# Score products on unpadded queries in four row groups, with the softmax of a half task re-cut, in a two-layer encoder on one Trainium2 core

## The chip, the cores and the metric

The kernel runs on one core of one Trainium2 chip (trn2). The metric is device time in microseconds of one execution. A run of the kernel gives one time; the time before is the median of three runs.

## The reference, cut to what matters

All of it is in float32. The trunk has two layers over 256 tokens (4 rows of 64) with 2048 channels; the change lies in the attention of the first.

```python
def neighbourhood_attention(h, w_qkv, b_qkv, w_o, rpb):
    qkv = (h @ w_qkv + b_qkv).reshape(B, S, 3, N_HEADS, HEAD_DIM)   # 64 heads of 32
    q = qkv[:, :, 0] * (HEAD_DIM ** -0.5)
    ...
    def row_block(r):                                               # 4 rows of 64 queries
        ...
        bias = rpb[:, dr_idx[None, :, None], dc_idx[:, None, :]]
        s = jnp.einsum('bqhd,bkhd->bhqk', qb, kb) + bias[None]
        s = jnp.where(mask[None, None], s, neg)                     # 16 columns around the query
        pr = jax.nn.softmax(s, axis=-1)
        return jnp.einsum('bhqk,bkhd->bqhd', pr, vb)
    ...
    return o @ w_o

def reference(x, p, ...):
    for i in range(DEPTH):                                          # 2
        if i % 2 == 0: x = x + neighbourhood_attention(rms_norm(x, ...), ...)
        else:          x = x + multiscale_pool(rms_norm(x, ...), ...)
        x = x + swiglu(rms_norm(x, ...), ...)                       # D_FF 5632
        gate = sigmoid(rms_norm(x, ...) @ w_ple_gate[i] + b_ple_gate[i])
        x = x + (p[i] @ w_ple_proj[i]) * gate
    return rms_norm(x, final_norm_g)
```

## The kernel before, in words

Activations lie transposed, channels on the 128 partitions and the 256 tokens along the free axis. To keep float32 accuracy on TensorE, each activation and each weight is split into a high and a low part (`at`, `wh`, `wl`), and `product` (from line 326) multiplies high by both parts of the activation (512 columns, L336) and low by the high one (256 columns, L340).

Weights stream from HBM in chunks of 1 MB on SP's queue, into three raw buffers. `Weights.make` (L94, L95) turns a chunk into two halves of `wh` (a cast on ScalarE) and `wl` (a subtraction on VectorE). There are four slots for halves, so two chunks; `get` makes sure that the two chunks after the one in use are made. All large products take their chunks in one fixed order.

The attention goes through four groups g of 16 heads. For each group `qk` computes queries and keys (eight chunks), `v_proj` the values (four chunks), and from g = 1 on `out_proj(g - 1)` adds the group before to x (four chunks); `out_proj(3)` comes last. A group's 16 heads are four tasks f of four heads j. The 256 queries are taken in four blocks b of 64 (4 rows by 16 columns), each against a window of 4 rows by 32 columns of keys, so 128 keys.

The small work of a task hangs between the chunks. `Side` is a queue of functions, each with a count of steps to let pass; `product` makes a step after every accumulator (8 pairs of products), `v_proj` after every 12 products. `queue_scores` puts the four `scores` tasks between the products of `v_proj`; `queue_attend` puts the transposes of the probabilities (`prob_t`) and the products with the values (`attend`) between the products that follow: of `qk(1, 0)` for g = 0, of `out_proj(g - 1)` for the others.

In `scores` a query tile `qz_f` holds for each head j the 128 channels of f with all but head j's 32 rows zero (filled with zeros once, L409; four activations of 32 partitions write the diagonal, L444). For each pair pr of blocks eight products (L496) go to one PSUM bank of the pool `pt` (`tmp_ps`, two buffers, shared with the transposes and the attend outputs): the two blocks in the two halves of the partitions, the four heads side by side. GpSimd adds bias and mask (L490, four additions, two buffers); VectorE adds them to the scores (L501), takes the maximum (L505) and the reciprocal of the sum (L512); ScalarE takes the exponential with the sum beside it (L508); GpSimd scales (L513). Accumulators of the large products (`acc`) are a pool of their own: three buffers of two PSUM banks.

Which instruction stands where on an engine is decided by the Tile framework's scheduler, by priority and dependence; `urgent()` raises the priority of what is issued within it. Each engine then works through its list in order.

Of the kernel before, what the change touches and what calls it, by code (L numbers as in the profile page):

```python
# [8 lines left out]
F32 = mybir.dt.float32  # L9
# [5 lines left out]
P = 128  # L15
# [115 lines left out]
def tile_encoder(  # L131
# [251 lines left out]
    def attention(nxt):  # L383
# [43 lines left out]
        def qk(g, kind):  # L427
# [26 lines left out]
        def v_proj(g):  # L454
# [17 lines left out]
            for t in range(2):  # L472
                nc.vector.scalar_tensor_tensor(v[:, t, :], a[:, t, :], norm.rows[:, t : t + 1], vb, ALU.mult, ALU.add)
# [9 lines left out]
        def scores(g, f, pr):  # L483
            rb = rb_tiles[g]
            bm = ap2.tile([P, 4, 4, 32], F32, tag="bm", name=f"bm_{g}_{f}_{pr}")
            off = 8 if pr == 0 else 0
            base = rb[:, f * 4 : f * 4 + 4, off : off + 1]
            for j in range(4):
                w1 = bass.AP(tensor=base.tensor, offset=base.offset + j * RUN, ap=[list(base.ap[0]), [31, 4], [1, 32]])
                nc.gpsimd.tensor_tensor(bm[:, j], w1, mask[:, pr : pr + 1, :].broadcast_to([P, 4, 32]), ALU.add)  # L490
            sp = tmp_ps(f"s_{g}_{f}_{pr}")
            for j in range(4):
# [433 lines left out]
```

## Time and profile before

| | us |
|---|---|
| three runs | 2183.17, 2184.16, 2184.46 |
| median | 2184.16 |
| profiled execution, its own time | 2185.78 |
| its span, first to last instruction | 2184.0 |

| engine | busy, share of the span |
|---|---|
| TensorE (PE) | 98% |
| weight load into it (PEld) | 86% |
| VectorE (DVE) | 62% |
| ScalarE (ACT) | 50% |
| GpSimd (POOL) | 9% |

The granted TensorE clock is 0.995 of full speed on average. The attention fills the first 440 us or so, a fifth of the span; the rest is the two feed-forward stages, the gated embeddings and the pooling mixer, which the change does not touch. In a profile PE's busy time counts pipelined products that overlap, so within a stage the distance from one start to the next tells more than the length of one instruction. Times below are microseconds from the span's start.

### The profile page before, as it was taken

What the parts mean: (1) busy time and instruction counts of PE and PEld (TensorE: products, weight loads), DVE (VectorE), ACT (ScalarE), POOL (GpSimd) and SP (SyncE); (2) the same over time, 40 slices, a digit from 0 to 9 for tenths busy, and PEclk for the clock granted to TensorE, in tenths of its full rate; (3) what the DMA queues carried; (4) which work ended last, traced back from release to release, by engine and by line L of the source; (5) the groups of instructions that cost most, each with busy time, mean ns of one, the idle gap of its engine ahead of it and who ended that gap; (6) DMA issues with size and microseconds to landing.
All of it is one profiled execution on the core that took longest, in us unless ns stands there. A gap on an engine that the chain in (4) does not pass through costs nothing.

```text
span 2184.0 us, 32133 instructions
## 1 busy us (share of the span) xinstructions
PE 2148.2 (98%) x13092; PEld 1874.3 (86%) x13092; DVE 1355.8 (62%) x1561; ACT 1088.0 (50%) x1554; POOL 185.7 (9%) x274
## 2 busy tenths in 40 slices
PE   7999999999999999999999999999999999999997
PEld 6888888888888888888888888888888888888887
DVE  5756575876555555566566677556555555556676
ACT  6665656654444434444445566444443344444453
POOL 3424132100000000000003100000000000000013
PEclk9999999999999999999999999999999999999999
DMA  8666565465555555555555454555555555555553
GB/s 243 183 190 190 180 180 174 155 205 191 193 184 184 191 192 184 184 192 192 186 184 184 171 193 141 187 185 183 193 193 183 184 192 193 183 185 192 193 174 116
DMA packets 209443, 402.92 MB, mean 184 GB/s; under 512 B 7936, under 2 KB 20352, under 8 KB 209296
## 3 DMA queue, kind: packets, MB, share of 16 engines
q1 hardware_dynamic: 206000, 393.38, 54.5%
q0 software_dynamic: 2192, 6.49, 1.6%
q8 instruction: 102, 1.67, 0.3%
q10 hardware_dynamic: 1104, 1.02, 0.1%
q14 instruction: 45, 0.37, 0.0%
HBM read 394.56 MB, written 2.10 MB: 182 GB/s over the span
## 4 chain that ended last, share of the span: by engine, by line
PE 95%; POOL 1%; DMA 1%; DVE 1%; issue 1%; ACT 1%; SPq 0%; POOLq 0%; DVEq 0%; ACTq 0%
PE ff L336 30%; PE ff L340 15%; PE dn L336 15%; PE dn L340 8%; PE qk L336 5%; PE pl L336 4%; PE qk L340 3%; PE pl L340 2%; PE wo L336 2%; PE v L466 1%; PE s L496 1%; PE v L468 1%; PE v L467 1%; PE wo L340 1%; PE wo L355 1%; PE ptp L522 1%
## 5 line engine op out<-in xcount | busy, mean ns | idle before, releaser
L95 DVE TENSOR_TENSOR wl<-raw,wh 128x1024 fp32r<-128x1024 f32 (+1 forms) x740 | 904.3, 1229 | 638.6 <-ACT wh L94 637.4
L94 ACT CAST wh<-raw 128x1024 fp32r<-128x1024 f32 (+1 forms) x740 | 768.7, 1043 | 806.5 <-PE ff L336 300.5
L336 PE MATMUL ff<-at_f,wh 128*128 128x512 f32 x2816 | 986.2, 394 | 0.0
L340 PE MATMUL ff<-at_f,wl 128*128 128x256 f32 x2816 | 790.4, 281 | 0.0
L336 PEld LDWEIGHTS ff<-at_f,wh 128*128 128x128 f32 x2816 | 529.6, 188 | 121.8
L340 PEld LDWEIGHTS ff<-at_f,wl 128*128 128x128 f32 x2816 | 530.3, 188 | 0.4 <-DVE wl L95 0.2
L336 PE MATMUL dn<-ht,wh 128*128 128x512 f32 x1408 | 493.0, 394 | 0.0
L340 PE MATMUL dn<-ht,wl 128*128 128x256 f32 x1408 | 395.3, 281 | 0.0
L336 PEld LDWEIGHTS dn<-ht,wh 128*128 128x128 f32 x1408 | 264.8, 188 | 61.1
L340 PEld LDWEIGHTS dn<-ht,wl 128*128 128x128 f32 x1408 | 265.1, 188 | 0.0
L336 PE MATMUL qk<-at_attn,wh 128*128 128x512 f32 x512 | 183.9, 402 | 12.1 <-ACT wh L94 6.5
L336 PE MATMUL pl<-at_p,wh 128*128 128x512 f32 x448 | 158.5, 397 | 0.0
L340 PE MATMUL qk<-at_attn,wl 128*128 128x256 f32 x512 | 144.9, 284 | 0.0
L340 PE MATMUL pl<-at_p,wl 128*128 128x256 f32 x448 | 126.3, 282 | 1.7 <-DVE wl L95 1.7
L336 PEld LDWEIGHTS qk<-at_attn,wh 128*128 128x128 f32 x512 | 97.7, 191 | 34.5 <-ACT wh L94 12.4
L336 PEld LDWEIGHTS pl<-at_p,wh 128*128 128x128 f32 x448 | 84.8, 189 | 19.4
L340 PEld LDWEIGHTS qk<-at_attn,wl 128*128 128x128 f32 x512 | 97.9, 191 | 1.7 <-DVE wl L95 1.2
L370 DVE TENSOR_TENSOR join_ff<-ff,lo_ff 128x512 f32<-128x512 f32 x88 | 60.4, 686 | 54.1 <-ACT lo_ff L368 54.1
L368 ACT COPY lo_ff<-ff 128x512 f32<-128x512 f32 x88 | 51.3, 583 | 81.9 <-PE ff L340 81.9
L304 POOL TENSOR_TENSOR tiny<-tiny 128x2 f32<-128x2 f32 x7 | 9.2, 1315 | 923.5 <-DVE tiny L302 923.5
L340 PEld LDWEIGHTS pl<-at_p,wl 128*128 128x128 f32 x448 | 84.9, 190 | 2.1 <-DVE wl L95 2.1
L490 POOL TENSOR_TENSOR bm<-rb,mask 128x128 f32<-128x128 f32 x128 | 67.6, 563 | 207.9 <-DVE p L501 174.7
(170 smaller groups left out, 1727.6 us busy)
## 6 DMA issues: line engine op xcount, KB each, us to landing
raw<-in_w_gate_dram SPq DMA_DIRECT2D x88, 1024.0 KB, 5.0
raw<-in_w_up_dram SPq DMA_DIRECT2D x88, 1024.0 KB, 5.0
raw<-in_w_down_dram SPq DMA_DIRECT2D x88, 1024.0 KB, 4.9
raw<-in_w_qkv_dram SPq DMA_DIRECT2D x46, 1024.0 KB, 5.2
raw<-in_w_ple_gate_dram SPq DMA_DIRECT2D x32, 1024.0 KB, 4.9
raw<-in_w_o_dram SPq DMA_DIRECT2D x16, 1024.0 KB, 4.9
rb<-in_rpb_dram POOLq DMA_DIRECT2D x32, 133.0 KB, 7.0
vw<-v SPq DMA_DIRECT2D x64, 64.0 KB, 2.7
```

Source lines behind the costliest of these rows:

```text
L94: self.nc.scalar.copy(wh[:, z], r)
L95: self.nc.vector.tensor_tensor(wl[:, z], r, wh[:, z].bitcast(F32), ALU.subtract)
L336: nc.tensor.matmul(a[:, f, :], lhsT=wh[:, k % per, c], rhs=v.rearrange("p a s -> p (a s)"), start=(first and k == 0), stop=False,)
L340: nc.tensor.matmul(a[:, f, :S], lhsT=wl[:, k % per, c], rhs=v[:, 0, :], start=False, stop=(last and k == nk - 1),)
L355: nc.tensor.matmul(o, lhsT=w[:, k % per, c], rhs=v[:, h, :], start=(first and k == 0 and n == 0), stop=(last and k == nk - 1 and n == 2),)
L368: nc.scalar.copy(lo, a[:, :, S:])
L370: nc.vector.tensor_tensor(s, a[:, :, :S], lo, ALU.add)
L466: nc.tensor.matmul(a[:, t, :], lhsT=hi, rhs=wh[:, k % 2, :], start=first, stop=False)
L467: nc.tensor.matmul(a[:, t, :], lhsT=hi, rhs=wl[:, k % 2, :], start=False, stop=False)
L468: nc.tensor.matmul(a[:, t, :], lhsT=lo, rhs=wh[:, k % 2, :], start=False, stop=last)
L490: nc.gpsimd.tensor_tensor(bm[:, j], w1, mask[:, pr : pr + 1, :].broadcast_to([P, 4, 32]), ALU.add)
L496: nc.tensor.matmul(sp[blk * 64 : blk * 64 + 64, j * P : (j + 1) * P], lhsT=qz[f][:, j, b * 64 : (b + 1) * 64], rhs=kv, start=True, stop=True,)
```

## The change

Queries are kept without padding: `qT_f` is one tile of 128 channels by 256, written by one activation, and a head's score product reads only its 32 partitions of `qT` and `kT`. `scores` issues all 16 products of a task at once, into two accumulators from `acc` (two heads each, a bank per head, both pairs of blocks side by side in the bank). The softmax runs per half task h (two heads, all four blocks) instead of per pair of blocks. Bias and mask take two additions of 256 elements, one for each pair of blocks, in four buffers. The additions to the scores, and those that make v, are urgent. Of the four score tasks the first waits for no step, where it waited for one; the transposes wait for four steps instead of two.

```diff
-        qz = []
-        for f in range(4):
-            z = ap_.tile([P, 4, S], F32, name=f"qz_{f}")
-            nc.gpsimd.memset(z, 0.0)
-            qz.append(z)
-        kT = [None] * 4
+        qT, kT = [None] * 4, [None] * 4
...
                     if kind == 0:
-                        for j in range(4):
-                            pr = slice(j * HD, (j + 1) * HD)
-                            nc.scalar.activation(
-                                qz[f][pr, j, :].rearrange("p (b r c) -> p r b c", b=4, r=4),
-                                reversed_last(sm[pr, f2, :].rearrange("p (r b c) -> p r b c", r=4, b=4)), AF.Identity,
-                                bias=bq_s[pr, b : b + 1], scale=float(HD) ** -0.5,
-                            )
+                        qt_ = ap_.tile([P, S], F32, tag=f"qT{f}", name=f"qT_{g}_{f}")
+                        nc.scalar.activation(
+                            qt_.rearrange("p (b r c) -> p r b c", b=4, r=4),
+                            reversed_last(sm[:, f2, :].rearrange("p (r b c) -> p r b c", r=4, b=4)), AF.Identity,
+                            bias=bq_s[:, b : b + 1], scale=float(HD) ** -0.5,
+                        )
+                        qT[f] = qt_
...
-            for t in range(2):
+            with urgent():
+              for t in range(2):
                 nc.vector.scalar_tensor_tensor(v[:, t, :], a[:, t, :], norm.rows[:, t : t + 1], vb, ALU.mult, ALU.add)
...
-        def scores(g, f, pr):
+        def scores(g, f):
             rb = rb_tiles[g]
...
-            sp = tmp_ps(f"s_{g}_{f}_{pr}")
-            for j in range(4):
+            sp = [acc(f"s_{g}_{f}_{h}") for h in range(2)]
+            for pr in range(2):
                 for blk in range(2):
                     b = 2 * pr + blk
-                    kv = kT[f].rearrange("p (r c) -> p r c", r=4)[:, :, KEY_LO[b] : KEY_LO[b] + 32]
-                    nc.tensor.matmul(
-                        sp[blk * 64 : blk * 64 + 64, j * P : (j + 1) * P], lhsT=qz[f][:, j, b * 64 : (b + 1) * 64],
-                        rhs=kv, start=True, stop=True,
-                    )
...
+                    for j in range(4):
+                        rows = slice(j * HD, (j + 1) * HD)
+                        kv = kT[f][rows].rearrange("p (r c) -> p r c", r=4)[:, :, KEY_LO[b] : KEY_LO[b] + 32]
+                        nc.tensor.matmul(
+                            sp[j // 2][blk * 64 : blk * 64 + 64, j % 2, pr * P : (pr + 1) * P],
+                            lhsT=qT[f][rows, b * 64 : (b + 1) * 64], rhs=kv, start=True, stop=True,
+                        )
+            for h in range(2):
+                softmax(g, f, h, sp[h], rb)
+
+        def softmax(g, f, h, sp, rb):
+            bm = ap2.tile([P, 2, 2, 4, 32], F32, tag="bm", bufs=4, name=f"bm_{g}_{f}_{h}")
+            n = f * 4 + h * 2
+            for p2 in range(2):
...
+                nc.gpsimd.tensor_tensor(bm[:, :, p2], near, ok, ALU.add)
+            s = ap3.tile([P, 4, P], F32, tag="prob", name=f"p_{g}_{f}_{h}")
+            with urgent():
+                nc.vector.tensor_tensor(
+                    s.rearrange("p (j b) k -> p j (b k)", j=2), sp[:, :, :S],
+                    bm.rearrange("p j b r c -> p j (b r c)"), ALU.add,
+                )
...
         def queue_scores(g):
             for f in range(4):
-                side.add(lambda f=f: (scores(g, f, 0), scores(g, f, 1)), 1)
+                side.add(lambda f=f: scores(g, f), 0 if f == 0 else 1)
...
-                side.add(lambda f=f: task(f), 2 if f == 0 else 0)
+                side.add(lambda f=f: task(f), 4 if f == 0 else 0)
```

`attend` now takes its probabilities from the half task of the head (`pv[j // 2]`) and goes through the blocks in the same order as before.

How instructions move, at three places. Names end with the group, the task and the half; the last number is a buffer's. First TensorE where the first score task of group 0 stands between the products for v. Before:

```order
L466 MATMUL v_0_662<-wh_8_1_564,at_attn_1_179 128x512
L467 MATMUL v_0_662<-wl_8_1_565,at_attn_1_179 128x512
L468 MATMUL v_0_662<-wh_8_1_564,at_attn_1_179 128x512
L496 MATMUL s_0_0_0_702<-kT_0_0_647,qz_0_226 64x128 x8
L496 MATMUL s_0_0_1_728<-kT_0_0_647,qz_0_226 64x128 x8
L466 MATMUL v_0_662<-wh_9_0_602,at_attn_2_184 128x512
L467 MATMUL v_0_662<-wl_9_0_603,at_attn_2_184 128x512
L468 MATMUL v_0_662<-wh_9_0_602,at_attn_2_184 128x512
```

Now:

```order
L461 MATMUL v_0_646<-wh_8_0_544,at_attn_0_162 128x512
L462 MATMUL v_0_646<-wl_8_0_545,at_attn_0_162 128x512
L463 MATMUL v_0_646<-wh_8_0_544,at_attn_0_162 128x512
L490 MATMUL s_0_0_0_669<-kT_0_0_631,qT_0_0_434 64x128 x5
L490 MATMUL s_0_0_1_670<-kT_0_0_631,qT_0_0_434 64x128 x4
L490 MATMUL s_0_0_0_669<-kT_0_0_631,qT_0_0_434 64x128
L490 MATMUL s_0_0_1_670<-kT_0_0_631,qT_0_0_434 64x128 x2
L490 MATMUL s_0_0_0_669<-kT_0_0_631,qT_0_0_434 64x128 x2
L490 MATMUL s_0_0_1_670<-kT_0_0_631,qT_0_0_434 64x128 x2
L461 MATMUL v_0_646<-wh_8_1_548,at_attn_1_179 128x512
L462 MATMUL v_0_646<-wl_8_1_549,at_attn_1_179 128x512
L463 MATMUL v_0_646<-wh_8_1_548,at_attn_1_179 128x512
```

The block stands 12 products of v earlier (before the second half of the chunk instead of after it), and its products change between the two accumulators of the halves; in the first task of a group the first five go to one of them. In the tasks f = 1 to 3 they change after every two, in the order of the loops.

Second VectorE through the second task of group 0, with the weight subtractions (`wl`) between. Before:

```order
L95 TENSOR_TENSOR wl_11_0_752<-raw_11_749,wh_11_0_751 128x1024
L95 TENSOR_TENSOR wl_11_1_756<-raw_11_749,wh_11_1_755 128x1024
L501 TENSOR_TENSOR p_0_1_0_797<-s_0_1_0_788,bm_0_1_0_783 128x512
L501 TENSOR_TENSOR p_0_1_1_823<-s_0_1_1_814,bm_0_1_1_809 128x512
L505 TENSOR_REDUCE mx_0_1_0_799<-p_0_1_0_797 128x4
L505 TENSOR_REDUCE mx_0_1_1_825<-p_0_1_1_823 128x4
L512 RECIPROCAL rc_0_1_0_806<-sm_0_1_0_801 128x4
L512 RECIPROCAL rc_0_1_1_832<-sm_0_1_1_827 128x4
```

Now:

```order
L511 TENSOR_TENSOR p_0_1_0_772<-s_0_1_0_751,bm_0_1_0_769 128x512
L511 TENSOR_TENSOR p_0_1_1_787<-s_0_1_1_752,bm_0_1_1_784 128x512
L95 TENSOR_TENSOR wl_11_0_732<-raw_11_729,wh_11_0_731 128x1024
L516 TENSOR_REDUCE mx_0_1_0_774<-p_0_1_0_772 128x4
L516 TENSOR_REDUCE mx_0_1_1_789<-p_0_1_1_787 128x4
L95 TENSOR_TENSOR wl_11_1_736<-raw_11_729,wh_11_1_735 128x1024
L523 RECIPROCAL rc_0_1_0_781<-sm_0_1_0_776 128x4
L523 RECIPROCAL rc_0_1_1_796<-sm_0_1_1_791 128x4
```

The two additions to the scores come first, and one of the two weight subtractions has moved between the maxima and the reciprocals.

Third TensorE at the end of the attention, around the last attend (`o_3_3`). Before:

```order
L336 MATMUL wo_2_3_0_4352<-oT_2_1_3008,wh_59_1_4151 128x512
L340 MATMUL wo_2_3_0_4352<-oT_2_1_3008,wl_59_1_4152 128x256
L535 MATMUL o_3_3_4380<-pT_3_3_0_4320,vw_3_4076 32x64 x8
L535 MATMUL o_3_3_4380<-pT_3_3_1_4346,vw_3_4076 32x64 x8
L336 MATMUL wo_2_3_1_4353<-oT_2_0_3007,wh_59_0_4147 128x512
L340 MATMUL wo_2_3_1_4353<-oT_2_0_3007,wl_59_0_4148 128x256
L336 MATMUL wo_2_3_1_4353<-oT_2_0_3007,wh_59_0_4147 128x512
```

Now:

```order
L533 MATMUL ptp_3_3_1_4285<-ident_60,p_3_3_1_3945 128x128 x4
L355 MATMUL wo_3_0_0_4315<-oT_3_0_3989,wh_60_0_4091 128x256 x2
L355 MATMUL wo_3_0_0_4315<-oT_3_0_3989,wl_60_0_4092 128x256
L355 MATMUL wo_3_0_0_4315<-oT_3_1_3990,wh_60_1_4095 128x256
L355 MATMUL wo_3_0_1_4316<-oT_3_0_3989,wh_60_0_4091 128x256 x2
L545 MATMUL o_3_3_4296<-pT_3_3_0_4264,vw_3_3972 32x64 x2
...
L545 MATMUL o_3_3_4296<-pT_3_3_1_4290,vw_3_3972 32x64 x2
L355 MATMUL wo_3_0_1_4316<-oT_3_0_3989,wl_60_0_4092 128x256
L355 MATMUL wo_3_0_1_4316<-oT_3_0_3989,wh_60_0_4091 128x256 x2
L355 MATMUL wo_3_0_0_4315<-oT_3_1_3990,wh_60_1_4095 128x256
```

It has moved from among the products of `out_proj(2)` (`wo_2`) to among the first products of `out_proj(3)` (`wo_3`).

## Rows read from the trace of the kernel before

**Rows 1.** The page: span, and busy time of each engine.
```profile
span 2184.0 us, 32133 instructions
...
PE 2148.2 (98%) x13092; PEld 1874.3 (86%) x13092; DVE 1355.8 (62%) x1561; ACT 1088.0 (50%) x1554; POOL 185.7 (9%) x274
```
**Rows 2.** The page: the chain that ended last, its shares by engine.
```profile
PE 95%; POOL 1%; DMA 1%; DVE 1%; issue 1%; ACT 1%; SPq 0%; POOLq 0%; DVEq 0%; ACTq 0%
```
**Rows 3.** Waits of PE, 0 to 560 us: total us, times, longest.
```profile
PE qk L336 <- ACT wh L94: 6.5, 1, 6.5
PE qk L336 <- DVE at_attn L255: 5.6, 1, 5.6
PE wo L340 <- issue: 1.8, 2, 1.2
PE ptp L522 <- ACT pT L524: 1.0, 4, 0.2
```
**Rows 4.** The chain in order of time: start us, us, what.
```profile
68.43 1.90 PE s L496 x32
...
115.45 0.58 PE o L535 x32
...
386.67 1.90 PE s L496 x32
...
458.96 0.45 PE bps_f L311 x4
```
**Rows 5.** Timeline, end of group 0's keys: start us, us, instruction.
```profile
62.61 0.28 PE L340 MATMUL qk<-at_attn,wl 128*128 128x256 f32 x1
...
65.37 0.68 DVE L370 TENSOR_TENSOR join_qk<-qk,lo_qk 128x512 f32<-128x512 f32 x1
```
**Rows 6.** Busy time by stretch: v stages of groups 0 and 3.
```profile
core 0: us, PE busy (x) PEld busy (x) DVE busy (x) ACT busy (x) POOL busy (x), PEclk, DMA share, GB/s
62.70:93.20 30.50, 30.50 (x226) 24.53 (x224) 21.09 (x31) 19.67 (x62) 18.40 (x31) 1.00 0.51 170
...
358.00:388.50 30.50, 30.50 (x227) 24.51 (x225) 21.15 (x31) 19.60 (x62) 18.27 (x30) 1.00 0.45 154
```
**Rows 7.** Groups of instructions, 0 to 560 us: busy us, mean ns, idle before.
```profile
L444 ACT ACTIVATE qz<-join_qk,cols 32x256 f32<-32x256 f32 x64 | 32.4, 506 | 1.6 <-DVE join_qk L437 0.8
L496 PE MATMUL s<-kT,qz 128*64 128x128 f32 x512 | 31.5, 276 | 0.0
L496 PEld LDWEIGHTS s<-kT,qz 128*64 128x64 f32 x512 | 27.6, 137 | 5.8 <-issue 5.8
```
**Rows 8.** Timeline of GpSimd at the start.
```profile
5.25 3.63 POOL L409 MEMSET qz<- 128x1024 f32 x4
```
**Rows 9.** Timeline of VectorE, second task of group 0; in brackets the idle time before.
```profile
76.19 2.58 DVE L95 TENSOR_TENSOR wl<-raw,wh 128x1024 fp32r<-128x1024 f32 x2 [0.76 <-ACT wh L94]
78.69 1.28 DVE L501 TENSOR_TENSOR p<-s,bm 128x512 f32<-128x512 f32 x2
79.89 1.26 DVE L505 TENSOR_REDUCE mx<-p 128x4 f32<-128x512 f32 x2
82.41 0.18 DVE L512 RECIPROCAL rc<-sm 128x4 f32<-128x4 f32 x1 [1.26 <-ACT p L508]
83.95 0.18 DVE L512 RECIPROCAL rc<-sm 128x4 f32<-128x4 f32 x1 [1.36 <-ACT p L508]
```
**Rows 10.** Timeline of ScalarE, second task: first exponential, and the casts after the eighth.
```profile
80.65 0.40 ACT L508 ACTIVATE p<-p,mx 128x128 f32<-128x128 f32 x1 [3.44 <-DVE mx L505]
...
83.75 1.98 ACT L94 CAST wh<-raw 128x1024 fp32r<-128x1024 f32 x2
```
**Rows 11.** Groups of instructions, 0 to 560 us: what follows transposes and attend.
```profile
L524 ACT COPY pT<-ptp 128x512 f32<-128x512 f32 x32 | 18.2, 582 | 15.8 <-PE ptp L522 15.8
...
L545 DVE TENSOR_TENSOR oT<-o,oT 128x256 fp32r<-128x256 f32 x16 | 6.7, 417 | 3.8 <-ACT oT L544 3.6
L544 ACT CAST oT<-o 128x256 fp32r<-128x256 f32 x16 | 6.0, 373 | 9.3 <-PE o L535 9.3
```

More of the change, by code (lines that the diff above doesn't have):

```diff
@@ L481, in attention @@
         probs = {}
-        def scores(g, f, pr):
+        def scores(g, f):
             rb = rb_tiles[g]
-            bm = ap2.tile([P, 4, 4, 32], F32, tag="bm", name=f"bm_{g}_{f}_{pr}")
-            off = 8 if pr == 0 else 0
-            base = rb[:, f * 4 : f * 4 + 4, off : off + 1]
-            for j in range(4):
-                w1 = bass.AP(tensor=base.tensor, offset=base.offset + j * RUN, ap=[list(base.ap[0]), [31, 4], [1, 32]])
-                nc.gpsimd.tensor_tensor(bm[:, j], w1, mask[:, pr : pr + 1, :].broadcast_to([P, 4, 32]), ALU.add)
-            sp = tmp_ps(f"s_{g}_{f}_{pr}")
-            for j in range(4):
+            sp = [acc(f"s_{g}_{f}_{h}") for h in range(2)]
+            for pr in range(2):
@@ L493, in scores @@
                 for blk in range(2):
                     b = 2 * pr + blk
-                    kv = kT[f].rearrange("p (r c) -> p r c", r=4)[:, :, KEY_LO[b] : KEY_LO[b] + 32]
-                    nc.tensor.matmul(
-                        sp[blk * 64 : blk * 64 + 64, j * P : (j + 1) * P], lhsT=qz[f][:, j, b * 64 : (b + 1) * 64],
-                        rhs=kv, start=True, stop=True,
-                    )
-            s = ap3.tile([P, 4, P], F32, tag="prob", name=f"p_{g}_{f}_{pr}")
-            nc.vector.tensor_tensor(
-                s, sp.rearrange("p (j k) -> p j k", j=4), bm.rearrange("p j a b -> p j (a b)"), ALU.add
-            )
@@ L504, in scores @@
-            mx = aps.tile([P, 4], F32, tag="mx", name=f"mx_{g}_{f}_{pr}")
+                    for j in range(4):
[5 more added lines that the diff above has]
+                        )
@@ new lines, in scores @@
+            for h in range(2):
[4 more added lines that the diff above has]
+            for p2 in range(2):
+                off = 8 if p2 == 0 else 0
+                base = rb[:, n : n + 1, off : off + 1]
+                near = bass.AP(
+                    tensor=base.tensor, offset=base.offset, ap=[list(base.ap[0]), [RUN, 2], [31, 4], [1, 32]]
+                )
+                ok = mask[:, p2 : p2 + 1, :].unsqueeze(1).broadcast_to([P, 2, 4, 32])
+                nc.gpsimd.tensor_tensor(bm[:, :, p2], near, ok, ALU.add)
[4 more added lines that the diff above has]
+                    bm.rearrange("p j b r c -> p j (b r c)"), ALU.add,
+                )
+            mx = aps.tile([P, 4], F32, tag="mx", name=f"mx_{g}_{f}_{h}")
@@ L505, in scores @@
             nc.vector.tensor_reduce(mx, s, AX.X, ALU.max, negate=True)
-            sm = aps.tile([P, 4], F32, tag="sm", name=f"sm_{g}_{f}_{pr}")
+            sm = aps.tile([P, 4], F32, tag="sm", name=f"sm_{g}_{f}_{h}")
             for j in range(4):
@@ L510, in scores, with prob_t @@
                 )
-            rc = aps.tile([P, 4], F32, tag="rc", name=f"rc_{g}_{f}_{pr}")
+            rc = aps.tile([P, 4], F32, tag="rc", name=f"rc_{g}_{f}_{h}")
             nc.vector.reciprocal(rc, sm)
             nc.gpsimd.tensor_tensor(s, s, rc.unsqueeze(2).broadcast_to([P, 4, P]), ALU.mult)
-            probs[f, pr] = s
+            probs[f, h] = s
         prob_ts = {}
-        def prob_t(g, f, pr):
-            s = probs.pop((f, pr))
-            tp = tmp_ps(f"ptp_{g}_{f}_{pr}")
+        def prob_t(g, f, h):
+            s = probs.pop((f, h))
+            tp = tmp_ps(f"ptp_{g}_{f}_{h}")
             for j in range(4):
                 nc.tensor.transpose(tp[:, j * P : (j + 1) * P], s[:, j, :], ident)
-            o = ap2.tile([P, 4, P], F32, tag="ptT", bufs=3, name=f"pT_{g}_{f}_{pr}")
+            o = ap2.tile([P, 4, P], F32, tag="ptT", bufs=3, name=f"pT_{g}_{f}_{h}")
             nc.scalar.copy(o, tp.rearrange("p (j k) -> p j k", j=4))
-            prob_ts[f, pr] = o
+            prob_ts[f, h] = o
         def attend(g, f):
             op = tmp_ps(f"o_{g}_{f}")
-            for pr in range(2):
-                pv = prob_ts.pop((f, pr))
-                for blk in range(2):
-                    b = 2 * pr + blk
-                    for j in range(4):
-                        h = f * 4 + j
-                        nc.tensor.matmul(
-                            op[j * HD : (j + 1) * HD, b * 64 : (b + 1) * 64],
-                            lhsT=vw_tiles[g][:, b, h * HD : (h + 1) * HD], rhs=pv[:, j, blk * 64 : blk * 64 + 64],
-                            start=True, stop=True,
-                        )
+            pv = [prob_ts.pop((f, h)) for h in range(2)]
+            for b in range(4):
+                pr, blk = b // 2, b % 2
+                for j in range(4):
+                    h = f * 4 + j
+                    nc.tensor.matmul(
+                        op[j * HD : (j + 1) * HD, b * 64 : (b + 1) * 64],
+                        lhsT=vw_tiles[g][:, b, h * HD : (h + 1) * HD],
+                        rhs=pv[j // 2][:, 2 * (j % 2) + pr, blk * 64 : blk * 64 + 64], start=True, stop=True,
+                    )
             o = oT[g][f // 2]
```

## The prediction

> **What bounds the kernel now.** I read the page's busy shares first. TensorE is busy 2148.2 of 2184.0 us [rows 1], and the chain that ended last runs 95% through it [rows 2]. The table of waits over the first 560 us, which hold the whole attention, then shows what keeps it from being busy: one wait of 6.5 us for a cast weight and one of 5.6 us for a split activation, both in the first query products, and 1.8 and 1.0 us in small pieces [rows 3]. So in the attention nothing else ends last: a microsecond of TensorE work taken out shortens the program by a microsecond, unless a new wait takes its place.
>
> The chain in order of time shows what the change works on. Between the products for v stand 16 blocks of score products, one for each f of each group g: 32 instructions in 1.90 us, the first block as the last [rows 4]. 16 x 1.90 = 30.4 us, 1.4% of the span. On its diagonal the kernel multiplies by zeros: each product uses all 128 rows of the array for the 32 that hold one head.
>
> **What 32 such instructions cost.** Each f32 product shows as two instructions. Three rows give the pace [rows 4]. With the whole array in use, four instructions of 128 columns take 0.45 us, 0.11 each. In a score block the output lies alternately in the upper and the lower half of the partitions; 32 instructions one at a time would be 32 x 0.11 = 3.5 us, two at a time 1.76, and the row says 1.90: two at a time, and 0.14 of filling. In attend the output lies in four groups of 32 partitions and there are 64 columns, so 0.055 each: four at a time 8 x 0.055 + 0.14 = 0.58, and the row says 0.58. So products that use different parts of the array run side by side, as many as there are parts.
>
> **The change, part by part.**
>
> *Score products.* 16 products a block as before, but each on 32 rows and 64 columns, so the array has 4 x 2 = 8 parts, and the four heads follow each other in four row groups. Eight at a time: 4 x 0.11 + 0.14 = 0.58 us, 1.32 less. No row of before has row groups: the bounds are 3.66 us (one at a time, 32 x 0.11 + 0.14) and 0.58. I take 0.58, since both forms that the trace has reach their full number of parts. Twelve blocks (f = 1 to 3) save 12 x 1.32 = 15.8 us. The Trainium skill (TensorE: Matmul & The Clock Gate, Part 3, on packing small matmuls) gives 3.07 times for four row groups of 512 columns; no run here shows it yet, and by it a block would cost 1.90 / 3.07 = 0.62, an estimate that lowers the sum by 0.6 us.
>
> *The first block of each group.* The first order piece shows it placed 12 products of v earlier and with its heads out of turn (five from the first accumulator, then four from the second): I count 6 rounds for 4, 0.80 us, saving 1.10. It now also needs both accumulators that the keys came from. The second is released by an addition that ends at 65.37 + 0.68 = 66.05, while the keys' last product starts at 62.61 [rows 5]; 12 products of v later (0.23 us each, from [rows 6]: (30.5 - 4 x 2.1) / 96) it is 65.4, and the five products from the first accumulator hide another 0.3. Wait: 0.3. Four groups save 4 x 0.8 = 3.2 us.
>
> *Queries.* Four activations of 32 partitions become one of 128: 64 x 506 ns [rows 7] become 16, so ScalarE loses 24 us of work. TensorE waited for none of it, so this is worth nothing by itself. The four fills with zeros go from GpSimd (3.63 us at 5.25 [rows 8]), so the bias loads behind them start that much earlier, next to the first weights. Both ways at most 3.6 us; I take zero, as the same bytes move before the first long wait ends.
>
> *Bias and mask.* 128 additions become 64 of double length on GpSimd, and four buffers replace two. GpSimd is busy 18.4 us of a v stage of 30.5 [rows 6]: nothing.
>
> *The softmax loop.* This is the cover to watch. In a v stage VectorE is busy 21.1 us and ScalarE 19.7 [rows 6]; with four blocks of 1.3 us out, the stage is 25.3 us and a block's period 6.3 instead of 7.6. VectorE works in order and stands waiting for the exponentials: from one block's weight subtraction at 76.19 to its second reciprocal's end at 84.13 it takes 7.9 us, 2.6 of them waiting [rows 9]. In that order it would not keep up with 6.3. But the second order piece shows a new one: a weight subtraction now stands between maximum and reciprocal, where VectorE waited. A loop is then two additions 1.28, a subtraction 1.22, the first maximum 0.63, and the eight exponentials 3.1 (80.65 to 83.75 [rows 10]), with the other maximum and subtraction beside them: 6.4 us with the reciprocals. That is 0.1 a block behind TensorE, and the weights are prepared two chunks ahead. ScalarE needs 3.1 + 2.0 a block. I cost it at nothing; if this cover fails it is the third rival.
>
> *v urgent.* The two additions now come before one maximum and one subtraction, and so the 16 copies of v on SP's queue and the weight loads behind them don't slip. Nothing.
>
> *Probability products two steps later.* The work is unchanged; each step is 8 pairs of products. The group's transposes and attends now run into the next query products' evacuation, in groups 1 to 3 into the last output products. The waits of this kind were 1.8 + 1.0 us [rows 3]; I take 1.5 us more, between 0 and 5. For the last group there is no later work to fill with: the third order piece shows the last attend inside the first product of out_proj(3), which needs its result. Between them stand a copy of 0.58, a cast of 0.37 and a subtraction of 0.42 [rows 11], 1.4 us with the handshakes more, of which half is covered by the products placed there: 1.0 us.
>
> **Sum.** 15.8 + 3.2 - 1.5 - 1.0 = 16.5 us. The profiled execution took 2185.78 (span 2184.0 and 1.8 around it), so 2169.3; it stands 1.6 above the median of the three runs, 2184.16. Against the median: **2168**. About 0.2%, 4 us, is what a measurement of this kernel can tell from no change.
>
> **The rivals.**
>
> *Half the width.* The weights of the four row groups might enter one after another, or a round take only one column half: 8 rounds, 1.02 us. For it: the weight loads of a score block already fill 27.6 of its 31.5 us [rows 7]. Against it: in attend four loads fit in each round. Saving 12 x 0.88 + 4 x 0.4 - 2.5 = 9.7 us: **2174**.
>
> *The softmax loop keeps its 7.9 us.* Then the fourth addition of each group comes 3 x (7.9 - 6.3) = 4.8 us late, the accumulators of the last scores are held, and the next projection's first product waits for them some 3 us, 12 in all, plus late weights: **2180 to 2184**. For it: every loop shows the two waits. Against it: the new order.
>
> *Row groups don't run side by side (slower).* Place: the score blocks. Neighbours today lie in different column halves; after the change four in a row lie in the same half and differ only in rows. If the array couldn't run those together, only the two places in a block where the half changes overlap, and 32 instructions take some 29 rounds, 3.3 us: 16 x 1.4 = 22 us and the 2.5 of waits on top, **2209**. It decides from fewer than two at a time on. Nothing in the trace excludes it, as no product there uses fewer than 128 rows; the exact fit of both other forms speaks against it.
>
> *Nothing gained.* If the two instructions of one product must follow each other and all start in program order, a round holds the second of one and the first of the next, two, however many parts there are: blocks stay at 1.90, and only the waits come: **2187**. The score rows fit this too; the attend row does not (17 rounds x 0.055 + 0.14 = 1.08, measured 0.58). The same skill page, in its list of what overlaps, says that matmuls start and end strictly in program order; by that rule this rival holds, and the attend row disagrees with it.
>
> **How the numbers follow.** Forecast 0.60 (2162 to 2173, by the bounds of the waits and of the first blocks), half width 0.17, the loop 0.10, no gain 0.07, slower 0.06. The range 2161 to 2179 holds the first two and the better part of the loop. Faster: 0.60 + 0.17 + 0.08 = 0.85; same: 0.02 + 0.07 = 0.09; slower 0.06.
>
> **What would show it.** Right: in the chain each score block shows 32 instructions in some 0.6 us, the first of a group 0.8 to 1.1; a v stage of 25 to 26 us; TensorE's waits in this table not over 18 us; VectorE's reciprocals waiting under 1.5 us a block. Half width shows as blocks of 1.0. The loop shows as TensorE waiting for the score additions or for weights at the first product after a v stage. Wrong altogether: blocks of 1.9 or more, or new idle time of TensorE of over 10 us.

## The result, and the profile after

The changed kernel took **2164.70 us** (median of 3 runs, 2164.41 to 2165.30) against 2184.16: a ratio of **0.9911, 95% interval [0.9897, 0.9925]**, 19.5 us less. The profiled execution took 2165.3, against 2185.78 before. The forecast was 2168 in a range from 2161 to 2179.

The page after (compare [rows 1]):

```profile
span 2163.6 us, 32007 instructions
...
PE 2130.9 (98%) x13092; PEld 1856.6 (86%) x13092; DVE 1354.4 (63%) x1561; ACT 1063.3 (49%) x1506; POOL 168.5 (8%) x206
```

TensorE is busy 17.3 us less, the span is 20.4 shorter. The chain in order of time (start us, us, what) shows the score blocks that [rows 4] had at 1.90:

```profile
64.99 1.12 PE s L490 x32
...
143.59 1.12 PE s L490 x32
...
150.48 0.62 PE s L490 x32
...
365.79 0.62 PE s L490 x32
```

12 x (1.90 - 0.62) + 4 x (1.90 - 1.12) = 15.4 + 3.1 = 18.5 us. The waits of TensorE, 0 to 560 us (compare [rows 3]):

```profile
PE qk L336 <- ACT wh L94: 5.8, 2, 5.1
PE qk L336 <- DVE at_attn L255: 5.5, 1, 5.5
PE wo L336 <- ACT wh L94: 1.6, 2, 0.8
```

The waits at the probability products (1.0) and for issue at the output products (1.8) are gone. The v stages of the four groups, by stretch (columns as in [rows 6]; the stretches begin 0.1 us after the first product):

```profile
62.16:88.88 26.72, 26.09 (x226) 19.72 (x225) 20.84 (x30) 19.43 (x62) 15.37 (x18) 1.00 0.62 169
140.77:167.68 26.91, 26.10 (x226) 19.73 (x225) 20.93 (x30) 19.42 (x62) 15.36 (x18) 1.00 0.60 168
242.06:268.97 26.91, 26.10 (x226) 19.73 (x225) 20.93 (x30) 19.43 (x62) 15.35 (x18) 1.00 0.57 169
343.38:369.30 25.92, 25.92 (x226) 19.88 (x225) 19.95 (x31) 19.25 (x61) 13.42 (x14) 1.00 0.49 163
```

They were 30.49 each. 25.92 in the last group is what the shorter blocks allow (30.49 - 4.62); groups 0 to 2 lose 0.8, 1.0 and 1.0 at their end. Here the chain leaves TensorE. In group 0 it reads:

```profile
74.06 0.68 DVE p L511
74.74 1.65 DVE wl L95
76.39 0.61 DVE mx L516
77.09 0.55 ACT p L519 x3
...
78.17 2.12 ACT p L519 x11
80.51 0.55 issue
81.05 0.68 DVE p L511
81.73 2.15 DVE wl L95
...
87.78 0.94 ACT wh L94
```

This is the softmax loop, and after it a cast of weights for which TensorE waits. Its period is in the timeline of VectorE and GpSimd (compare [rows 9]):

```profile
73.47 1.27 DVE L511 TENSOR_TENSOR p<-s,bm 128x512 f32<-128x512 f32 x2
74.66 1.74 DVE L95 TENSOR_TENSOR wl<-raw,wh 128x1024 fp32r<-128x1024 f32 x1
...
77.51 1.21 DVE L95 TENSOR_TENSOR wl<-raw,wh 128x1024 fp32r<-128x1024 f32 x1
...
80.48 1.26 DVE L511 TENSOR_TENSOR p<-s,bm 128x512 f32<-128x512 f32 x2
81.65 2.23 DVE L95 TENSOR_TENSOR wl<-raw,wh 128x1024 fp32r<-128x1024 f32 x1
...
87.97 1.26 DVE L511 TENSOR_TENSOR p<-s,bm 128x512 f32<-128x512 f32 x2
```
```profile
68.05 2.60 POOL L508 TENSOR_TENSOR bm<-rb,mask 128x256 f32<-128x256 f32 x4 [13.05 <-DVE p L511]
...
74.63 4.62 POOL L508 TENSOR_TENSOR bm<-rb,mask 128x256 f32<-128x256 f32 x4
79.55 1.19 POOL L419 DMA_DIRECT2D rb<-in_rpb_dram  x2 [0.29 <-POOL bm L508]
...
97.16 1.14 POOL L419 DMA_DIRECT2D rb<-in_rpb_dram  x2
```

From additions to additions it takes 7.01 and 7.49 us, where 6.4 was forecast and TensorE needs 6.35. A weight subtraction takes 1.2 us alone. The one inside the loop of 7.01 begins at 74.66, 0.03 us after a bias addition, and takes 1.74. The one inside the loop of 7.49 begins at 81.65, during GpSimd's two products with the reciprocals (80.75 to 82.80), and takes 2.23. GpSimd is held up in the same way. Four bias additions take 2.60 us alone and 4.62 beside subtractions, and of these four only the two that run into a subtraction are long. The last one is such: it begins 0.04 us after the subtraction at 77.51, which itself takes no more than 1.21:

```profile
77.55 1.70 POOL L508 TENSOR_TENSOR bm<-rb,mask 128x256 f32<-128x256 f32 x1
```

So whichever of the two begins second waits for the other. Groups 1 and 2 lose their 1.0 us at another place, in one subtraction of 2.84 us; in group 3 the same one takes 1.30 (group 1, then group 3):

```profile
158.34 1.18 POOL L419 DMA_DIRECT2D rb<-in_rpb_dram  x2 [0.29 <-POOL bm L508]
159.52 2.05 POOL L524 TENSOR_TENSOR p<-p,rc 128x512 f32<-128x512 f32 x2
159.82 2.84 DVE L95 TENSOR_TENSOR wl<-raw,wh 128x1024 fp32r<-128x1024 f32 x1
...
362.43 1.30 DVE L95 TENSOR_TENSOR wl<-raw,wh 128x1024 fp32r<-128x1024 f32 x1
```

There it is not the bias additions: the loop before this one has them beside it, and its subtractions take 1.22. GpSimd first issues two loads of the next group's bias, which keeps it for 1.18 us, so its two products begin just ahead of the subtraction, and that waits for both. Group 3 has no group behind it and loads nothing; its products begin at 360.60, early enough. In group 0 the two loads at 79.55 do the same to the loop of 7.49.

**The account.** Stages, from the start of a stage's first product to that of the next: the four v stages 15.5 us shorter (18.5 less the 2.8 lost to the loop and 0.2 that no row explains), the start to the first v stage 0.7, the stretches behind the v stages 0.4, 1.2, 1.5 and 0.5, the rest of the span, which the change does not touch, 0.6: 20.4. So two things were to be explained: the loop, forecast at nothing, and the stretches behind, forecast to lose 2.5 us and 3.6 us better.

### The profile page after: what moved, and what is told of

Same layout as the page of the kernel before. It is cut to its first block, busy times and chain, and to the rows that moved or that the text cites. A ratio compares the mean times of both kernels' runs of the same rounds, so it can differ in the third digit from the quotient of the medians.

```text
span 2163.6 us, 32007 instructions
## 1 busy us (share of the span) xinstructions
PE 2130.9 (98%) x13092; PEld 1856.6 (86%) x13092; DVE 1354.4 (63%) x1561; ACT 1063.3 (49%) x1506; POOL 168.5 (8%) x206
## 3 DMA queue, kind: packets, MB, share of 16 engines
q8 instruction: 102, 1.67, 0.3%
q10 hardware_dynamic: 1104, 1.02, 0.1%
## 4 chain that ended last, share of the span: by engine, by line
PE 94%; ACT 2%; DVE 1%; POOL 1%; issue 1%; DMA 1%; SPq 0%; POOLq 0%; DVEq 0%; ACTq 0%
PE ff L336 30%; PE ff L340 15%; PE dn L336 15%; PE dn L340 8%; PE qk L336 5%; PE pl L336 5%; PE qk L340 3%; PE pl L340 2%; PE wo L336 2%; PE wo L355 1%; PE wo L340 1%; PE v L461 1%; ACT p L519 1%; PE v L463 1%; PE v L462 1%
## 5 line engine op out<-in xcount | busy, mean ns | idle before, releaser
L336 PE MATMUL wo<-oT,wh 128*128 128x512 f32 x192 | 69.1, 401 | 1.6 <-ACT wh L94 1.6
```

Of the source, the lines that this page charges most:

```text
L336: nc.tensor.matmul(a[:, f, :], lhsT=wh[:, k % per, c], rhs=v.rearrange("p a s -> p (a s)"), start=(first and k == 0), stop=False,)
```

## The experiments

Twelve kernels, each the changed kernel with an edit, timed against the kernel before. Behind the ratio stand the v stages of groups 0 to 3, the stretch behind each of the first three (the next query and key products, from group 1 on with the output products ahead of them), and the median time from issue to landing of the weight loads that start between 88 and 120 us, the crossing from group 0 to 1. All in us, stages worked out from the starts of the products.

```
                      median   ratio [95%]              v stages                 behind v0, v1, v2     landing
before               2184.16                            30.5  30.5  30.5  30.5   52.3  75.6  75.9      9.0
changed              2164.70   0.9911 [0.9897, 0.9925]  26.7  26.9  26.9  25.9   51.9  74.4  74.4      5.3
x1_padded            2192.38   1.0036 [1.0023, 1.0048]  32.8  32.8  32.8  32.8   52.4  74.3  74.9      7.7
x11_padded_alternate 2183.84   0.9993 [0.9984, 1.0002]  30.7  30.7  30.7  30.7   52.5  74.5  74.5      7.6
x2_head_by_head      2168.07   0.9922 [0.9910, 0.9935]  27.0  27.0  27.0  26.1   52.0  74.4  74.8      5.3
x3_ptp_two           2172.52   0.9943 [0.9929, 0.9957]  26.7  26.9  26.9  25.9   56.0  75.2  75.2      6.9
x9_bm_two            2173.00   0.9947 [0.9934, 0.9959]  26.3  25.9  25.9  25.9   55.2  76.3  77.6      8.5
x12_bm_two_no_reload 2162.63   0.9897 [0.9883, 0.9910]  26.3  25.9  25.9  25.9   51.9  74.3  74.3      5.4
x10_half_bm          2173.57   0.9954 [0.9942, 0.9966]  25.9  25.9  25.9  25.9   55.6  76.7  74.3     11.7
x5_max_urgent        2167.31   0.9925 [0.9912, 0.9938]  26.9  27.0  27.0  26.5   51.9  74.6  74.6      5.2
x6_max_exp_urgent    2184.66   0.9999 [0.9991, 1.0008]  29.4  29.6  29.6  28.9   54.6  76.2  76.1      5.9
x8_no_max            2170.48   0.9944 [0.9932, 0.9956]  27.5  27.6  27.7  27.5   52.2  74.6  78.3      5.3
x13_bias_late        2169.71   0.9932 [0.9918, 0.9945]  25.9  26.9  27.9  28.4   51.8  74.3  74.4      5.3
x14_bias_mid         2163.02   0.9899 [0.9883, 0.9916]  25.9  26.0  25.9  25.9   51.8  74.3  74.3      7.1
```

### The row groups, and the order of the products

x1_padded has `qz` with its zeros and its activations back, and two bias buffers:

```diff
-                        kv = kT[f][rows].rearrange("p (r c) -> p r c", r=4)[:, :, KEY_LO[b] : KEY_LO[b] + 32]
+                        kv = kT[f].rearrange("p (r c) -> p r c", r=4)[:, :, KEY_LO[b] : KEY_LO[b] + 32]
...
-                            lhsT=qT[f][rows, b * 64 : (b + 1) * 64], rhs=kv, start=True, stop=True,
+                            lhsT=qz[f][:, j, b * 64 : (b + 1) * 64], rhs=kv, start=True, stop=True,
```

> The changed kernel with the padded queries back: each score product on all 128 rows again, four activations of 32 partitions for the queries; two additions, order and later probability products stay as changed, with two bias buffers since the padded queries take the room (the run with two buffers alone is its control). Theory, the row groups are the gain: score blocks go back from 0.62 (first of a group 1.12) to some 1.9 us, 12 x 1.28 + 4 x 0.78 = 18.5 us more; the stages of v, now 26.7 to 26.9 in groups 0 to 2, lose their waits for the softmax loop (2.8 us), as a block's period is 7.6 again: 2164.7 + 18.5 - 2.8 = 2180, ratio to before 0.997 to 0.999. Rival, the time came from the queries' activations, the additions or the later probability products, and the short blocks only uncover waits: 2165 to 2172.

x11_padded_alternate is the same with the order of before:

```diff
-                for blk in range(2):
-                    b = 2 * pr + blk
-                    for j in range(4):
+                for j in range(4):
+                    for blk in range(2):
+                        b = 2 * pr + blk
```

> The padded run again (two bias buffers, everything else as changed), but with its 16 score products written as in the kernel before: the two column halves in turn, where the padded run had four products of one half in a row and blocks of 2.50 us (2.38 the first). Theory, run-ahead past a product whose part is taken is limited when all share their rows: blocks 1.90, 12 x 0.60 + 4 x 0.48 = 9.1 us less than the padded run's 2192.4: 2182 to 2185; against the run with two buffers alone (2173.0) the row groups are then worth 9 to 12 us in this kernel, not 18.5, because the longer v stages hide transfers. Rival, the order does not matter: blocks 2.5, 2191 to 2194.

x2_head_by_head keeps the row groups and puts the loop over `j` outermost:

```diff
-            for pr in range(2):
-                for blk in range(2):
-                    b = 2 * pr + blk
-                    for j in range(4):
+            for j in range(4):
+                for pr in range(2):
+                    for blk in range(2):
+                        b = 2 * pr + blk
```

> The same 16 score products a block, written head by head: four products follow each other in one row group (two column halves in turn), then the next row group. Theory, matmuls start strictly in program order and one waits while its part of the array is taken: two at a time, 16 rounds of 0.11 + 0.14 = 1.9 us a block, 12 x 1.28 + 4 x 0.8 = 18.5 us more less 2.8 of loop waits, 2180. Rival, products run ahead to whichever part is free: blocks stay at 0.6, 2163 to 2167.

One later block each, from the chains of x1, x11 and x2:

```profile
75.06 2.50 PE s L495 x32
```
```profile
73.93 1.90 PE s L495 x32
```
```profile
71.97 0.67 PE s L490 x32
```

x1 came out 12 us above its number, and the blocks account for some 9 of them: 2.50 us instead of 1.90. Four padded products in a row for one column half no longer pair up fully; with the halves in turn (x11) the block is 1.90 and the time fell by 8.5 us, as the second expectation had it. So x11 is the clean undo. It lies within 0.1% of the kernel before: **without the row groups and the queries that go with them, the rest of the change (with two bias buffers) is worth nothing that can be measured**, and from x11 to x9, which has the same two buffers, the two together bring 10.8 us. In the v stages alone they bring 18.7 (122.8 to 104.1 in sum); the rest is given back outside them.

x2 decides on program order. Four products that share their rows follow each other there, in two column halves; if each waited for the one before it, two would run at a time, and a block would take 1.9 us. It takes 0.67 against 0.62. Products run ahead past others whose part of the array is taken, in row groups over a whole head, so TensorE does not keep to the order of its list, as the section on the kernel has it of every engine. The Trainium skill (TensorE: Matmul & The Clock Gate, Part 3) says that matmuls start and end strictly in program order; the 0.67 disagrees. Its 3.07 times for four row groups, given for products of 512 columns, agrees with 1.90 / 0.62 = 3.06 here, with 128. Why padded products run ahead less (2.50) stays open.

### Two steps later

```diff
-                side.add(lambda f=f: task(f), 4 if f == 0 else 0)
+                side.add(lambda f=f: task(f), 2 if f == 0 else 0)
```

> The probability products two steps after the drain as before, all else as changed. Stages behind the v stages became 0.4 + 1.2 + 1.5 + 0.5 + 0.5 = 4.1 us shorter, where 2.5 us longer were forecast. Theory, this is the later start (TensorE's waits of 1.8 and 1.0 us at the probability products and the output products are gone because of it): 2167.5 to 2169. Rival 1, the prediction's term (later costs 2.5 us): 2162. Rival 2, the waits went because ScalarE has 24 us less work on queries: within 1 us of 2164.7.

7.8 us more than the changed kernel: the first theory's sign, and twice its size. TensorE's wait in the first 560 us, and the windows in which the first attend falls (behind the length stands TensorE's busy time; the third number from the end is the granted clock):

```profile
PE o L545 <- DMA vw<-v: 2.9, 3, 2.1
```
```profile
102.50:104.00 1.50, 0.00 (x0) 0.00 (x0) 0.88 (x1) 0.11 (x1) 1.35 (x2) 0.99 1.04 246
104.00:105.50 1.50, 1.45 (x11) 1.19 (x12) 0.00 (x0) 0.00 (x0) 1.50 (x3) 0.50 1.01 363
105.50:107.00 1.50, 1.50 (x7) 1.34 (x6) 0.00 (x0) 0.00 (x0) 1.50 (x3) 0.50 1.05 406
```

The first attend stands waiting for the copies of v, 2.1 us, and then the granted clock is at 0.50, the lower level, for 3 us; in the changed kernel these windows have 1.00 throughout. The sixteen copies are issued one after another on SP's queue, from 91.65 to 101.8 us. In the kernel before they began 1.0 us before the end of the v stage (92.20, end 93.2), in the changed one 2.8 us after it (end 88.88), since the additions that make v stand behind the softmax loop on VectorE. The stretch behind v0 is 4.1 us longer by it. Two steps later is what lets the copies land. By the traces 6.0 us of the difference lie in the attention and 1.2 in later stages, which the edit does not touch.

### The bias buffers

```diff
-            bm = ap2.tile([P, 2, 2, 4, 32], F32, tag="bm", bufs=4, name=f"bm_{g}_{f}_{h}")
+            bm = ap2.tile([P, 2, 2, 4, 32], F32, tag="bm", bufs=2, name=f"bm_{g}_{f}_{h}")
```

> The changed kernel with two bias buffers instead of four. Theory: GpSimd writes a half task's bias well before VectorE reads it, and the buffers don't matter: 2163 to 2167. Rival: with two, GpSimd must wait for the score addition of the block before, falls behind and makes the softmax loop longer: the v stages 27 to 29 instead of 26.7, 2168 to 2172.

x12 adds to that:

```diff
         def load_bias(g):
+            if g > 0:
+                rb_tiles[g] = rb_tiles[0]
+                return
```

> The run with two bias buffers, but the bias of heads 0 to 15 is loaded once and used in all four groups (the reloads for groups 1 to 3 are left out, so these groups' scores have another bias). Theory, two buffers cost 8.3 us because the bias tile is given back later, so its reload falls beside the copies of v and the next weight load (8.5 us instead of 5.2): without reloads the stage behind the first v stage goes back from 55.2 to 52 us, that behind the third from 31.2 to 28, and the time to 2163 to 2166. Rival, GpSimd's additions themselves are late: 2171 to 2174.

x9 took 8.3 us more, though not as the rival said: the v stages got shorter, not longer. What it lost lies behind them. (By the spans of the traces the difference is 5.7 us; the runs of x9 spread from 2171.06 to 2177.03.) GpSimd's loads of x9, and a piece of its chain:

```profile
85.28 1.18 POOL L419 DMA_DIRECT2D rb<-in_rpb_dram  x2 [0.29 <-POOL bm L508]
...
96.40 2.24 POOL L419 DMA_DIRECT2D rb<-in_rpb_dram  x4
```
```profile
101.08 8.52 DMA raw<-in_w_qkv_dram
109.68 1.06 ACT wh L94
```

With two buffers the last additions of a group come later, so the bias tile is given back at 85 instead of 79 us, and four of its eight loads, not two, are issued beside the copies of v (90.89 to 101). The weight load behind those copies then takes 8.52 us instead of 5.3. TensorE waits in this stretch twice, 1.5 us each time: for the copies of v themselves, and for a copy of transposed probabilities on ScalarE, which stands there waiting to cast the late weights. x12 takes the reloads away and changes nothing else in the program: 10.4 us less than x9, landings of 5.4, and stretches behind the v stages as short as any. **So four buffers pay by when they let a transfer start**, not by what they save GpSimd.

### The softmax loop

The edits of x10, x5 (x6 has a `with urgent():` around the exponentials too) and x8:

```diff
-            bm = ap2.tile([P, 2, 2, 4, 32], F32, tag="bm", bufs=4, name=f"bm_{g}_{f}_{h}")
...
-                nc.gpsimd.tensor_tensor(bm[:, :, p2], near, ok, ALU.add)
+            if h == 0:
+                bm = ap2.tile([P, 2, 2, 4, 32], F32, tag="bm", bufs=4, name=f"bm_{g}_{f}_{h}")
...
+                    nc.gpsimd.tensor_tensor(bm[:, :, p2], near, ok, ALU.add)
+                bms[0] = bm
+            bm = bms[0]
```
```diff
-            nc.vector.tensor_reduce(mx, s, AX.X, ALU.max, negate=True)
+            with urgent():
+                nc.vector.tensor_reduce(mx, s, AX.X, ALU.max, negate=True)
```
```diff
-            nc.vector.tensor_reduce(mx, s, AX.X, ALU.max, negate=True)
...
-                    s[:, j, :], s[:, j, :], AF.Exp, bias=mx[:, j : j + 1], accum_out=sm[:, j : j + 1]
+                    s[:, j, :], s[:, j, :], AF.Exp, scale=0.01, accum_out=sm[:, j : j + 1]
```

> The changed kernel with only half of GpSimd's bias additions: the second half task of a block uses the bias of the first (its own heads' bias is left out). Theory, VectorE's subtractions are slow (1.74 and 2.23 us) because GpSimd adds the bias at the same time: they become 1.22 to 1.5, the loop 6.4 to 6.7, the v stages 26.0 to 26.3, the time 2162.5 to 2163.5. Rival, they are slow for another reason (loads that land): they stay at 1.7 to 2.2 and the time within 1 us of 2164.7.

> The changed kernel with the two maxima of a half task's softmax ahead of the weight subtractions on VectorE, as the two score additions already are. In the changed kernel a subtraction stands between additions and maxima, and takes 1.74 to 2.23 us beside GpSimd's bias additions, 1.22 else; the loop takes 7.0 and 7.5 us against a block's period on TensorE of 6.35. Theory, this loop holds up the v stages of groups 0 to 2 (26.7 to 26.9 us against 25.9): without the subtraction in the chain a loop is 5.3 to 5.9 us, the v stages become 25.9 to 26.2 and the time 2162 to 2163. Rival, the wait behind the v stage is for a weight that is late for another reason (its load): stages stay at 26.7 to 26.9, 2164 to 2166.

> As the run before, and the exponentials on ScalarE also ahead of the casts of weights. Theory, the loop: no more to win once it is under 6.35 us, 2162 to 2163. Rival, the casts on ScalarE are then late and TensorE waits for weights at the v products: 2165 to 2169.

> The changed kernel without the maxima: the exponentials are of the scores times 0.01, so the softmax is another one; 32 reductions of 0.63 us leave VectorE and the chain from additions to exponentials. Theory, the softmax loop costs the 2.8 us of the v stages: it falls to 5.7 to 6.2 us, the v stages to 25.9, the time to 2161.5 to 2163. Rival, the loop costs nothing and the weights' loads do: 2164 to 2166.

x10 has v stages of 25.9 in all groups, as its theory said, and is 8.9 us slower than the changed kernel all the same: its reload came at 91 to 99.7 us, in the midst of the copies, and the weights landed after 11.7 us. It does not show that theory, though, since the reload left the v stages together with half of the additions, and in group 0 the subtraction that begins behind an addition still took 1.73 us. x12 separates the two: its v stages have the additions and no reload. In its group 1 a subtraction of the loop, with an addition behind it:

```profile
158.31 1.26 DVE L95 TENSOR_TENSOR wl<-raw,wh 128x1024 fp32r<-128x1024 f32 x1
```

In its groups 1 to 3 the stages are 25.9, and group 0, where two subtractions begin behind an addition, has 26.3. So of the 2.8 us that the loop cost the changed kernel, the additions account for some 0.4, and the rest goes with the place of the bias loads; x9, whose loads come later, has the stages of x12.

x5, x6 and x8 missed. All three take work out of the chain or put it earlier, and all three made the v stages longer. x5's chain shows where its time goes:

```profile
79.52 0.95 ACT wh L94
80.49 2.29 DVE wl L95
82.78 1.20 DVE p L511 x2
```

With the maxima early, the weight subtractions of a block stand after them, and the next additions wait behind a subtraction that itself waits for a cast of weights on ScalarE (loops of 9.3 and 5.4 us, where the changed kernel has 7.01 and 7.49). x6 and x8 show the same pair ahead of their additions, with loops of 8.3 and 7.6 us (x6) and 6.7 and 7.0 (x8). In all three that subtraction also runs beside GpSimd's products, and takes 2.29 us (x5), 2.28 (x6) and 1.67 (x8). A subtraction between additions and maxima costs the chain 1.2 us or more, but it waits for no cast.

### Both at once

x13 keeps the order of the changed kernel, and takes the bias out of the v stages:

```diff
+            if g > 0:
+                nc.gpsimd.tensor_copy(rb[:, 0, 0:1], qT[3][:, 0:1])
...
-            bm = ap2.tile([P, 2, 2, 4, 32], F32, tag="bm", bufs=4, name=f"bm_{g}_{f}_{h}")
+            bm = ap2.tile([P, 2, 2, 4, 32], F32, tag="bm", bufs=8, name=f"bm_{g}_{f}_{h}")
```

x14 holds the loads on an earlier tile instead:

```diff
-                nc.gpsimd.tensor_copy(rb[:, 0, 0:1], qT[3][:, 0:1])
+                nc.gpsimd.tensor_copy(rb[:, 0, 0:1], oT[g - 1][0][:, 1, 0, 0:1].bitcast(F32))
```

> The changed kernel with eight bias buffers, and the bias reload of a group held until the group's queries are there (one column copied from the last query tile into the bias tile on GpSimd, ahead of the loads): the loads fall into the query and key products, and all bias additions stand before the v stage. Theory, additions beside the softmax loop lengthen it and reloads beside the v copies and weight loads cost what is saved there: VectorE's subtractions in the v stage are 1.22 us, the v stages of groups 1 to 3 25.9, and nothing is given back: 2160.5 to 2163. Rival, the reload in the query stage delays weight loads there or the bias comes late for the first score addition: 2165 to 2175.

> As the run with the bias late, but the reload is held on the attend of the group's f = 1 instead of the next queries: at 112.66 us instead of 119.55 in the changed kernel's time for the first, some 30 us earlier for the others. In the run before, group 0's v stage was 25.93 us as expected, but the loads of groups 1 to 3 landed 8 to 11.3 us after their issue and the 16 additions (16 us) ran into the v stages (26.86, 27.94, 28.41). Theory: with loads in the quiet stretch and all additions done before the v stages, these are 25.9 in every group and nothing is given back: 2160.5 to 2163, below the changed kernel's 2164.7. Rival, the loads now delay the weights of the query products: those stages over 46.5 (52.0 in group 1), 2165 to 2170.

x13 was half right: 25.9 in group 0, but the loads of the later groups came too late and the additions ran into the stages (up to 28.4). x14 mends that. Its GpSimd, its loop in group 0 and all its waits of TensorE from 0 to 560 us:

```profile
112.37 4.52 POOL L421 DMA_DIRECT2D rb<-in_rpb_dram  x8 [0.30 <-POOL rb L412]
123.82 15.68 POOL L510 TENSOR_TENSOR bm<-rb,mask 128x256 f32<-128x256 f32 x16 [6.93 <-DMA rb<-in_rpb_dram]
```
```profile
72.94 1.27 DVE L513 TENSOR_TENSOR p<-s,bm 128x512 f32<-128x512 f32 x2
74.13 1.22 DVE L95 TENSOR_TENSOR wl<-raw,wh 128x1024 fp32r<-128x1024 f32 x1
...
79.42 1.26 DVE L513 TENSOR_TENSOR p<-s,bm 128x512 f32<-128x512 f32 x2
```
```profile
PE qk L336 <- ACT wh L94: 5.6, 1, 5.6
PE qk L336 <- DVE at_attn L255: 5.5, 1, 5.5
```

The subtraction takes 1.22, the loop 6.48, the v stages 25.9 to 26.0, and only the two waits at the start are left. Its span is 2160.8 against 2163.6, its median 2163.02; the intervals of the two ratios overlap, so that it beats the changed kernel is read from the profile, not from the times.

## Why the prediction was right, point by point

- **Score blocks**: 15.8 forecast, 15.4 measured. The argument from the three rows of [rows 4], as many products at once as the array has parts, held; the half-width rival (1.02) and the one on program order (1.90) fell with the blocks of 0.62.
- **First blocks**: 3.2 forecast, 3.1 measured (1.12, where 0.80 and a wait of 0.3 were expected). x2, whose order is another, has 1.14, so how much of it is order and how much is wait isn't shown.
- **The softmax loop**: forecast at nothing, cost 2.8. The step that failed is "a subtraction 1.22": that is what it takes alone. Behind a bias addition of GpSimd it took 1.74, and behind products that the bias loads had put off 2.23 and 2.84. That it can take longer could have been seen: ten subtractions of the kernel before took 1.35 us each on average between 60 and 100 us. With additions and loads away from it the loop is 6.48 (x14), the 6.4 of the prediction. The sign named for this rival, TensorE waiting for weights at the first product after a v stage, is there with 0.6 us in group 0 and 0.8 in groups 1 and 2, not 3 a group.
- **Probability products two steps later**: forecast at -1.5 and -1.0. This step failed in its sign. The stretches behind the v stages became 3.6 us shorter, and back at two steps the kernel is 7.8 us slower (x3). The prediction saw where the work goes to, but not what it has to wait for where it was: copies of v, which the shorter stage and the in-order VectorE make late.
- **Bias and mask: nothing.** Wrong for the buffers: 8.3 us (x9, x12). The prediction said GpSimd had time; it did not ask when the bias tile comes free and where its reload then falls, on GpSimd's list and on the DMA queues.
- **Queries, fills, the order of the additions for v**: forecast at nothing. The start to the first v stage is 0.7 us shorter; no run separates these.

The total, -16.5 against -20.4, hides this: the loop's 2.8 and the 6.1 of the later products have opposite signs, so that it came this near is in part luck. With two bias buffers the row groups brought some 11 us, and without the later start the change loses 7.8: two other parts kept the rest from being given back.

## What to carry to other kernels

Where TensorE is the bound, its work taken out comes off the span only if every transfer that was paced by the longer stage still lands in time: ask of each buffer when it now comes free, and what its reload then meets on the DMA queues. An edit that looks free (two more buffers, a start two steps later) can be what makes the main one pay, so test it alone. And an engine that works in order is tuned by what each instruction waits for, on other engines too, not by the length of its chain: three edits that shortened the chain here made it slower.

## What the hardware did that was not expected

- Products in row groups run ahead past a whole head's products of the same rows (0.67 against 0.62); padded ones for one column half do so only in part (2.50 against 1.90).
- VectorE's subtraction of two SBUF operands and GpSimd's additions and products hold each other up, and the one that begins second waits: the subtraction took 1.74 us behind an addition and up to 2.84 behind two products instead of 1.2, and an addition that began behind a subtraction took 1.70 instead of 0.65. The score additions (1.26, one operand from PSUM) and the maxima (1.27) in the same stretch are not held up. The Trainium skill (SBUF — State Buffer, Who interferes with whom) says that a VectorE instruction with two SBUF inputs contends with a GpSimd instruction that reads SBUF, and one with a single such input does not; the rows agree.
- Bias loads and copies of v keep the DMA engines full at 110 to 160 GB/s (x10, 95 to 107.5 us: share 0.99 to 1.11), where weight loads alone move some 400 (105 to 110 us of the changed kernel: 408). With all eight bias loads (1 MB) issued beside the copies, the weight loads behind them landed after 11.7 us instead of 5.3 (medians, x10 and the changed kernel).
- After one wait of 2.1 us the granted clock was at 0.50 for the next 3 us (x3); after a wait of 2.0 us at the same products it stayed at 1.00 (x10, 105 to 110 us).
